# A LayerNorm one chunk later, three PSUM pairs and an earlier first weight slice in the first stage of an eight-core Trainium2 kernel

## Chip, cores and metric

The kernel runs on all eight cores of one Trainium2 chip. Each core does the same program on its own sequence. The time is device microseconds (us) of the slowest core. Most runs agree within 0.3%. Some runs fall into a slower state, in which some cores show a lower granted clock (0.811 to 0.959 where the fast runs show 0.984 to 0.997) and the time is longer (a run of before with cores 2 and 3 at 0.958 and 0.959 took 862.52 us, where the fast median was 838.60; its slowest, with cores 4 to 7 at 0.815 to 0.841, took 990.49); those runs are listed but not compared. A "fast run" below is one outside that state.

## The reference, cut to what matters

One layer of a decoder. Only its first step matters here: RMSNorm of the input, the projection `v`, Gelu, and a LayerNorm of the result, for 2,112 rows per core. The change is about the order in which that is done.

```python
h = rms_norm(x, norm_g)                       # x: 2048 + 64 rows of 1024 per core
z = jnp.einsum('bld,de->ble', h, w_in)        # split into u, v, gates, ...
v_a = layer_norm(jax.nn.gelu(v_a), ln_v_g, ln_v_b)
s = chunk_spatial_mix(v_a, w_s, b_s)          # within chunks of 128 rows
y_a = gelu(u_a) * s * silu(gate_a)
# ... branch B, the merge, the output projection and the embedding: not touched
```

## The kernel before: the parts that matter

The first stage takes the rows in 17 chunks of 128 (the last has 64). One chunk passes through every engine. The names below are used through the whole text.

```python
def A0(c):      # ScalarE: square of x with its sum ("square c"); POOL: add, pow -> RMSNorm factor ("rstd c")
def A2(c):      # VectorE: x * rstd * norm_g -> bf16                          ("scale c")
def A3(c):      # TensorE: 8 transposes into one PSUM bank
def A4(c):      # VectorE: copy of that bank into HT                          ("HT copy c")
def Bmm(c, slots):                    # TensorE: 4 matmuls for each slot (a slice of w_v): 16 in all
def Bact_g(c):  # ScalarE: Gelu of the PSUM pair, with its sum                ("Gelu c")
def Bact_s(c):  # ScalarE: square of that, with its sum
def C1(c):      # VectorE: three 1-element steps: mean, mean^2 - eps, variance ("the scalars")
def C2(c):      # POOL:    pow(variance, -1/2), one element per row           ("the pow")
def C3(c):      # VectorE: one 1-element step, then the normalise, 1024 wide
# C1, C2 and C3 are the LayerNorm of a chunk, "LN c".
```

The helper `S.op`, on which these functions rest, adds the semaphore waits that the data need. What an engine has to do is called its queue here, and the order of these calls in the program is taken as the order in each queue. PSUM is what the traces call `ps`, where every matmul of these traces puts its result (`MATMUL ps<-WR,HT`); a pair is two of its banks. `okc(c)` says that chunk c exists.

```python
        for i in range(4, NCH + 5):
            if 5 <= i - 1 < NCH:
                A2(i - 1)
            if 3 <= i - 3 < NCH:
                Bmm(i - 3, (0, 1))
            if 4 <= i - 2 < NCH:
                A3(i - 2)
                A4(i - 2)
            if 3 <= i - 3 < NCH:
                Bmm(i - 3, (2, 3))
            if okc(i - 5):
                C1(i - 5)
                C2(i - 5)
            if okc(i - 4):
                Bact_g(i - 4)
            if 5 <= i + 1 < NCH:
                A0(i + 1)
            if okc(i - 4):
                Bact_s(i - 4)
            if okc(i - 5):
                C3(i - 5)
            # ... loads cut
            if i == 13:
                S.op("dve", CP(Bd[:, :], ps[3][:, :]), reads=[B_bank[6], B_bank[7]], writes=[B_Bd])
            if i == 12:
                make_Bd()      # 16 small matmuls into ps[3], used later
                # ... loads cut
```

After this loop the second stage begins. It starts with the projection of `u` ("u-projection"), whose TensorE work needs all HT copies. Later, its products with `VA` need every LN.

Of the kernel before, what the change touches and what calls it, by code (L numbers as in the profile page):

```python
# [15 lines left out]
NCH = 17  # L16
# [145 lines left out]
def CP(out, in_):  # L162
    return lambda e: e.tensor_copy(out=out, in_=in_)  # L163
# [4 lines left out]
def DMA(out, in_):  # L168
    return lambda e: e.dma_start(out=out, in_=in_)  # L169

def build_program(stop_after=99, dbg=()):
# [31 lines left out]
    with ExitStack() as es:  # L203
# [90 lines left out]
        def warm(n):  # L294
            S.group("pe", [MM(ps[2][:, 512:1024], JUNK[:, 0:128], JUNK[:, 0:512], True, True) for _ in range(n)], reads=[B_junk])
# [58 lines left out]
        def A0(c):  # L354
            r, sl, hs = crow(c), c % NXI, c % 3
            S.op("act", ACT(HTOK[hs][0:r, :], XIN[sl][0:r, :], AF.Square, scale=1.0 / 32, accum_out=st(c, 0, r)),
                 reads=[B_xin[sl]], writes=[B_htok[hs], B_stat[c]])
            S.op("pool", TT(st(c, 1), st(c, 0), cc(C_EPS), ALU.add), reads=[B_cst], writes=[B_stat[c]])
            S.op("pool", TT(st(c, 2), st(c, 1), cc(C_NH), ALU.pow), reads=[B_cst], writes=[B_stat[c]])

        def A2(c):
            r, sl, hs = crow(c), c % NXI, c % 3
            S.op("dve", STT(HTOK[hs][0:r, :], XIN[sl][0:r, :], st(c, 2, r), BC0[0:r, :], ALU.mult, ALU.mult),
                 reads=[B_xin[sl], B_stat[c]] + B_bc0h, writes=[B_htok[hs]])

        def A3(c):
            r, sl, hs = crow(c), c % 2, c % 3
            pt = bank_bf(sl)
            S.group("pe", [TR(pt[:, k * 128:k * 128 + r], HTOK[hs][0:r, k * 128:(k + 1) * 128], ident[0:r, 0:r])
                           for k in range(8)], reads=[B_htok[hs], B_identb], writes=[B_bank[sl]])  # L370

        def A4(c):
            r, t0, sl = crow(c), c * 128, c % 2
            pt = bank_bf(sl)
            S.op("dve", CP(HT3[:, :, t0:t0 + r], pt.rearrange("p (k t) -> p k t", t=128)[:, :, 0:r]),
                 reads=[B_bank[sl]], writes=[B_hT[c]])

        def v_pair(c):
            return 1 + c if c < 3 else 1 + (c + 1) % 2

        def Bmm(c, slots=(0, 1, 2, 3)):
            r, t0, pi = crow(c), c * 128, v_pair(c)
            fns = [MM(ps[pi][0:r, q * 512:(q + 1) * 512], HT[:, k * NT + t0:k * NT + t0 + r],
                      WR[:, k * D + q * 512:k * D + (q + 1) * 512], k == 0, k == 7)
                   for s_ in slots for k in (2 * s_, 2 * s_ + 1) for q in range(2)]
            if slots[0] == 0:
                S._waits("pe", (), [B_bank[2 * pi], B_bank[2 * pi + 1]])
            S.group("pe", fns, reads=[B_hT[c]] + [B_ring[s_] for s_ in slots],
                    writes=[B_bank[2 * pi], B_bank[2 * pi + 1]] if slots[-1] == 3 else [])

        def Bact_g(c):
            r, pi, gs = crow(c), v_pair(c), c % 4
            S.op("act", ACT(GV[gs][0:r, :], ps[pi][0:r, :], AF.Gelu_apprx_tanh, accum_out=st(c, 3, r)),
                 reads=[B_bank[2 * pi], B_bank[2 * pi + 1]], writes=[B_gv[gs], B_stat[c]])

        def Bact_s(c):
            r, gs = crow(c), c % 4
            gv = GV[gs]
            S.op("act", ACT(JUNK[0:r, :], gv[0:r, :], AF.Square, accum_out=st(c, 4, r)),
                 reads=[B_gv[gs]], writes=[B_junk, B_stat[c]])  # L400

        def C1(c):
            r = crow(c)
            S.op("dve", TS(st(c, 5, r), st(c, 3, r), INVD, None, ALU.mult), writes=[B_stat[c]])
            S.op("dve", TS(st(c, 6, r), st(c, 5, r), st(c, 5, r), -LN_EPS, ALU.mult, ALU.add), writes=[B_stat[c]])
            S.op("dve", STT(st(c, 9, r), st(c, 4, r), INVD, st(c, 6, r), ALU.mult, ALU.subtract), writes=[B_stat[c]])

        def C2(c):
            S.op("pool", TT(st(c, 10), st(c, 9), cc(C_NH), ALU.pow), reads=[B_cst], writes=[B_stat[c]])
# [3 lines left out]
        def make_Bd():  # L413
            for q in range(2):
                fns = []
                for h in range(4 * q, 4 * q + 4):
                    o = ps[3][:, h * 128:(h + 1) * 128]
                    fns.append(MM(o, BC2b[:, h * 128:(h + 1) * 128], wT[:, h * 128:(h + 1) * 128], True, False))
                    fns.append(MM(o, ones[0:1, :], bsr[0:1, h * 128:(h + 1) * 128], False, True))
                S.group("pe", fns, reads=[B_bc2b, B_wT, B_ones, B_bsr], writes=[B_bank[6 + q]])  # L420

        def C3(c):
            r, gs = crow(c), c % 4
            gv = GV[gs]
            va = VA[0:r, c * D:(c + 1) * D]
            S.op("dve", STT(st(c, 12, r), st(c, 5, r), -1.0, st(c, 10, r), ALU.mult, ALU.mult), writes=[B_stat[c]])
            S.op("dve", TS(va, gv[0:r, :], st(c, 10, r), st(c, 12, r), ALU.mult, ALU.add),
                 reads=[B_stat[c], B_gv[gs]], writes=[B_va[c]])
            if c >= 15:
                S.op("dve", TS(gv[0:r, :], gv[0:r, :], st(c, 10, r), st(c, 12, r), ALU.mult, ALU.add),  # L430
                     reads=[B_stat[c]], writes=[B_gv[gs]])
                S.op("dve", TT(gv[0:r, :], gv[0:r, :], BC1[0:r, :], ALU.mult), reads=[B_bc1], writes=[B_gv[gs]])
                S.op("dve", TT(gv[0:r, :], gv[0:r, :], BC2[0:r, :], ALU.add), reads=[B_bc2], writes=[B_gv[gs]])
                dst = vp_d if c == 15 else vs_d
                ob = Buf("vout%d" % c)
                S.dma("sp", [DMA(dst[:, :], gv[0:r, :])], ob, reads=[B_gv[gs]])
                out_bufs.append(ob)

        def okc(c):
            return 0 <= c < NCH  # L440
# [13 lines left out]
                 writes=[B_bc0h[q]])  # L454
        warm(9)
        A2(0)
        A2(1)
        A3(0)
        A4(0)
        A3(1)  # L460
        A4(1)
        for s_ in range(2):
            for c in range(2):
                Bmm(c, (s_,))
        A2(2)
        A3(2)
        A4(2)
# [10 lines left out]
        A2(3)  # L478
        for c in range(3):
            Bmm(c, (2,))  # L480
        A0(4)
        Bmm(0, (3,))
        Bmm(1, (3,))
        A3(3)
        A4(3)
        Bmm(2, (3,))
        A2(4)
        for i in range(4, NCH + 5):
            if 5 <= i - 1 < NCH:
                A2(i - 1)  # L490
            if 3 <= i - 3 < NCH:
# [3 lines that stand above are left out]
                A4(i - 2)  # L495
            if 3 <= i - 3 < NCH:
                Bmm(i - 3, (2, 3))
            if okc(i - 5):
                C1(i - 5)
                C2(i - 5)  # L500
            if okc(i - 4):
                Bact_g(i - 4)
            if 5 <= i + 1 < NCH:
                A0(i + 1)
            if okc(i - 4):
                Bact_s(i - 4)
            if okc(i - 5):
                C3(i - 5)
            if NXI + 3 <= i + 5 < NCH:
                x_load(i + 5)  # L510
            if i == 9:
                S.op("pool", lambda e: e.affine_select(out=wT3, in_=WST.rearrange("s (h t) -> s h t", t=128),
                                                       pattern=[[0, 8], [1, 128]], compare_op=ALU.is_ge, fill=0.0,
                                                       base=0, channel_multiplier=-1),
                     reads=[B_ws], writes=[B_wT])
                issue_loads(6)
            if i == 11:
                issue_loads(NRING)
            if i == 10:
                S.op("dve", CP(BC2b, BC2), reads=[B_bc2], writes=[B_bc2b])  # L520
            if i == 13:
                S.op("dve", CP(Bd[:, :], ps[3][:, :]), reads=[B_bank[6], B_bank[7]], writes=[B_Bd])
            if i == 12:
                make_Bd()
                S.dma("sp", [DMA(BC1, ln_g_d.partition_broadcast(128))], B_bc1, writes=[B_bc1])
                S.dma("pool", [DMA(WPP[:, :].rearrange("p (k c) -> p k c", c=D),
                                   w_pp_d.rearrange("(k p) c -> p k c", p=128))], B_wpp, writes=[B_wpp])
            if i == 14:
                emit_blk_dmas()
                S.dma("sp", [DMA(ci_s[:, :], ci0_d[:, :])], B_cis[0], writes=B_cis)  # L530
# [495 lines left out]
```

## Time and profile before

| | before |
|---|---|
| time, median of 3 runs | 838.74 us (838.24 to 839.37) |
| spans of the eight cores in the profiled run | 832.9 to 836.9 us, mean 834.8 |
| u-projection starts, mean of the cores | 98.0 us |

How to read the lines: in a page, each engine has its busy time, the share of the span and the number of instructions. In the chain of waits (the line with shares only) each part of the span goes to the engine that the end of the program had to wait for. PE is TensorE, DVE is VectorE, ACT is ScalarE, POOL is GpSimd. The page of the kernel before, the slowest core (core 7):

```profile
span 836.9 us, 14194 instructions; the slowest of 8 cores (832.9 to 836.9 us)
...
PE 810.0 (97%) x4569; PEld 431.7 (52%) x4569; DVE 445.8 (53%) x726; ACT 301.0 (36%) x517; POOL 116.6 (14%) x257
...
PE 88%; DMA 3%; issue 3%; DVE 3%; ACT 1%; POOL 1%; DVEq 0%; POOLq 0%; SPq 0%; ACTq 0%
```

TensorE is busy 97% of the time. The rest must be sought where TensorE waits. All but 3.8 us of its waiting (on core 7) is in the first stage. In the list of waits of core 3 (columns: waited for, us in total, times, longest) its largest entry is this:

```profile
PE ps L143 <- DVE stat L159: 6.7, 10, 2.4
```

"DVE stat L159" is the VectorE instruction that began when the wait ended (at 34.88 us, for a matmul at 35.11). What TensorE needs is the end of the one before it, an HT copy (34.28 to 34.96). The timeline of core 3 shows it. Its columns are start, length, engine, line, operation, output, input, shape, count, and in brackets the idle time of the engine before it with what ended it. TensorE of before:

```profile
30.79 1.89 PE L143 MATMUL ps<-WR,HT 128*128 128x512 bf16 x8
35.11 1.89 PE L143 MATMUL ps<-WR,HT 128*128 128x512 bf16 x8 [2.43 <-DVE stat L159]
...
39.43 1.89 PE L143 MATMUL ps<-WR,HT 128*128 128x512 bf16 x8 [0.26 <-DVE stat L159]
...
43.75 1.89 PE L143 MATMUL ps<-WR,HT 128*128 128x512 bf16 x8 [0.26 <-DVE stat L159]
```

TensorE waits 2.43 us once, at chunk 4, and then 0.26 us per chunk. The first instructions of successive chunks (35.11, 39.43, 43.75) lie 4.32 us apart. VectorE of before, on the same core:

```profile
30.55 0.15 DVE L159 TENSOR_SCALAR stat<-stat 128x1 f32<-128x1 f32 x1 [0.70 <-ACT SCR L149]
30.81 0.21 DVE L160 TENSOR_SCALAR stat<-stat 128x1 f32<-128x1 f32 x1
31.13 0.16 DVE L155 SCALAR_TENSOR_TENSOR stat<-stat 128x1 f32<-128x1 f32 x1
32.09 0.16 DVE L155 SCALAR_TENSOR_TENSOR stat<-stat 128x1 f32<-128x1 f32 x1 [0.80 <-POOL stat L152]
32.35 0.81 DVE L160 TENSOR_SCALAR VA<-YA,stat 128x1024 bf16<-128x1024 f32 x1
33.08 1.28 DVE L155 SCALAR_TENSOR_TENSOR YA<-MG,stat 128x1024 bf16<-128x1024 f32 x1
34.28 0.68 DVE L163 COPY HT<-ps 128x1024 bf16<-128x1024 bf16 x1
...
38.60 0.68 DVE L163 COPY HT<-ps 128x1024 bf16<-128x1024 bf16 x1
...
72.15 0.69 DVE L163 COPY HT<-ps 128x1024 bf16<-128x1024 bf16 x1 [6.08 <-PE ps L146]
...
74.30 0.16 DVE L155 SCALAR_TENSOR_TENSOR stat<-stat 128x1 f32<-128x1 f32 x1 [0.82 <-POOL stat L152]
...
75.30 1.22 DVE L163 COPY Bd<-ps 128x1024 f32<-128x1024 f32 x1
```

The first three lines are the scalars of LN 0. They waited 0.70 us for ScalarE's square. Then VectorE stands still for 0.80 us until POOL has done the pow (32.09). Normalise (32.35), scale 5 (33.08) and HT copy 4 (34.28) come behind it. TensorE's matmul at 35.11 is released by that copy. HT copy 5 follows at 38.60. The last three lines are from the stretch in which TensorE makes `Bd`: VectorE is idle 6.08 us. Only then, in the next iteration, it waits 0.82 us for the pow of LN 8 and copies `Bd` for 1.22 us.

### The profile page before, as it was taken

To read this page: it belongs to the slowest core of one execution; us is meant where nothing else is said; L and a number is where in the kernel's file an instruction comes from. 1 tells how busy PE (TensorE), PEld (TensorE's weight loads), DVE (VectorE), ACT (ScalarE), POOL (GpSimd) and SP (SyncE) were. 2 spreads that over 40 slices of the span, in tenths; PEclk is the share of its full clock that TensorE was granted. 3 is DMA by queue.
4 is the path that set the end of the run, shared out by engine and by line. 5 is a ranking of instruction groups with operands and counts; after the bars stand their busy time and mean duration, and the time that the engine had idled before them with its cause. 6 is when DMAs were issued, how large, how long until landed. Compare 5 with 4: busy or idle time off the path is not lost.

```text
span 836.9 us, 14194 instructions; the slowest of 8 cores (832.9 to 836.9 us)
## 1 busy us (share of the span) xinstructions
PE 810.0 (97%) x4569; PEld 431.7 (52%) x4569; DVE 445.8 (53%) x726; ACT 301.0 (36%) x517; POOL 116.6 (14%) x257
## 2 busy tenths in 40 slices
PE   6899999999999999999999999999999999999994
PEld 2445455555554555455555545554555454444441
DVE  4575666546565555555555322232333246777774
ACT  2675554554432332232332111111111115555552
POOL 4342210000000100101001001000010013323331
PEclk8998999999999999999999999999999999999998
DMA  8977072311300410600602406006023563444311
GB/s 180 237 178 144 1 151 39 51 24 29 51 1 1 71 31 1 101 1 2 101 1 48 86 1 101 2 0 101 2 39 62 83 171 126 142 142 143 120 76 63
DMA packets 21338, 60.78 MB, mean 73 GB/s; under 512 B 2770, under 2 KB 7058, under 8 KB 21268
## 3 DMA queue, kind: packets, MB, share of 16 engines
q0 software_dynamic: 10352, 29.89, 21.5%
q1 hardware_dynamic: 10914, 29.99, 11.5%
q8 instruction: 40, 0.66, 0.3%
q14 instruction: 30, 0.25, 0.1%
q10 hardware_dynamic: 2, 0.00, 0.0%
HBM read 78.08 MB, written 9.58 MB: 105 GB/s over the span
## 4 chain that ended last, share of the span: by engine, by line
PE 88%; DMA 3%; issue 3%; DVE 3%; ACT 1%; POOL 1%; DVEq 0%; POOLq 0%; SPq 0%; ACTq 0%
PE ps L143 86%; DMA MG<-x 2%; PE ps L146 1%; DMA YA<-pe_g 1%; POOL stat L152 1%; DVE HT L163 1%; DVE YA L155 1%; ACT YA L149 0%; ACT SCR L149 0%; DVE stat L155 0%; DVE MG L155 0%; DVE stat L160 0%; ACT MG L149 0%; POOL WR L169 0%; DVE YA L152 0%
## 5 line engine op out<-in xcount | busy, mean ns | idle before, releaser
L143 PE MATMUL ps<-HT,WR 128*128 128x512 bf16 (+2 forms) x2560 | 469.7, 342 | 0.0
L143 PEld LDWEIGHTS ps<-HT,WR 128*128 128x128 bf16 x2560 | 248.4, 98 | 200.7 <-issue 0.4
L149 ACT ACTIVATE SCR<-ps 128x512 f32<-128x512 f32 (+2 forms) x240 | 123.7, 520 | 324.1 <-PE ps L143 274.0
L155 DVE SCALAR_TENSOR_TENSOR SCR<-SCR,ps 128x512 f32<-128x512 f32 (+2 forms) x80 | 47.6, 594 | 151.1 <-PE ps L143 151.1
L152 POOL TENSOR_TENSOR stat<-stat,cst 128x1 f32<-128x1 f32 x119 | 68.2, 576 | 175.3 <-ACT SCR L149 102.9
L143 PE MATMUL ps<-WR,HT 128*128 128x512 bf16 (+1 forms) x272 | 68.8, 404 | 6.6 <-DVE stat L159 5.5
L152 DVE TENSOR_TENSOR SCR<-SCR,ps 128x512 f32<-128x512 f32 (+2 forms) x88 | 48.2, 547 | 46.3 <-PE ps L143 38.5
L155 DVE SCALAR_TENSOR_TENSOR SCR<-SCR,cpks 128x512 f32<-128x512 f32 (+1 forms) x80 | 51.6, 645 | 37.6 <-ACT SCR L149 27.8
L143 PE MATMUL ps<-HT 128*128 128x512 bf16 (+1 forms) x272 | 61.6, 379 | 2.3 <-ACT HT L149 2.3
L143 PE MATMUL ps<-YA,WR 128*128 128x512 bf16 (+2 forms) x320 | 63.6, 342 | 0.0
L143 PE MATMUL ps<-VA,WR 128*128 128x512 bf16 (+2 forms) x320 | 63.6, 342 | 0.0
L169 POOL DMA_DIRECT2D WR<-wt x44 | 24.0, 546 | 274.2 <-PE ps L143 272.4
L143 PE MATMUL ps<-WR,MG 128*128 128x512 bf16 (+1 forms) x272 | 61.3, 379 | 0.0
L143 PEld LDWEIGHTS ps<-WR,HT 128*128 128x128 bf16 (+1 forms) x272 | 26.6, 103 | 40.9 <-issue 18.1
L149 ACT ACTIVATE SCR<-SCR,cpks 128x512 f32<-128x512 f32 (+1 forms) x40 | 25.5, 637 | 60.5 <-DVE SCR L152 60.5
L152 DVE TENSOR_TENSOR SCR<-SCR 128x512 f32<-128x512 f32 (+2 forms) x40 | 23.7, 593 | 41.3 <-ACT SCR L149 41.3
L143 PEld LDWEIGHTS ps<-YA,WR 128*128 128x128 bf16 x320 | 31.3, 98 | 25.8
L143 PEld LDWEIGHTS ps<-VA,WR 128*128 128x128 bf16 x320 | 31.3, 98 | 25.8
L143 PEld LDWEIGHTS ps<-WR,MG 128*128 128x128 bf16 (+1 forms) x272 | 26.7, 99 | 31.7 <-issue 0.4
L143 PEld LDWEIGHTS ps<-HT 128*128 128x128 bf16 (+1 forms) x272 | 26.0, 99 | 31.1 <-issue 3.3
L155 DVE SCALAR_TENSOR_TENSOR YA<-YA,ps 128x1024 f32<-128x1024 f32 (+1 forms) x17 | 20.7, 1220 | 21.7 <-ACT YA L149 21.7
L152 DVE TENSOR_TENSOR VA<-SCR 128x512 bf16<-128x512 f32 (+2 forms) x48 | 25.3, 526 | 8.1 <-DVE SCR L152 4.8
(85 smaller groups left out, 549.2 us busy)
## 6 DMA issues: line engine op xcount, KB each, us to landing
WR<-wt POOLq DMA_DIRECT2D x44, 512.0 KB, 10.2
y<-YA SPq DMA_DIRECT2D x16, 512.0 KB, 2.9
MG<-x SPq DMA_DIRECT2D x12, 512.0 KB, 7.8
WR<-x SPq DMA_DIRECT2D x8, 512.0 KB, 4.8
VA<-x SPq DMA_DIRECT2D x8, 512.0 KB, 4.4
WR<-w_v POOLq DMA_DIRECT2D x4, 512.0 KB, 11.6
MG<-x POOLq DMA_DIRECT2D x4, 512.0 KB, 13.4
SCR<-p SPq DMA_DIRECT2D x16, 128.0 KB, 4.3
```

Of the source, the lines that this page charges most:

```text
L143: return lambda e: e.matmul(out, lhsT=lhsT, rhs=rhs, start=start, stop=stop)
L146: return lambda e: e.transpose(out, in_, idn)
L149: return lambda e: e.activation(out=out, in_=in_, func=func, **kw)
L152: return lambda e: e.tensor_tensor(out=out, in0=in0, in1=in1, op=op)
L155: return lambda e: e.scalar_tensor_tensor(out=out, in0=in0, scalar=scalar, in1=in1, op0=op0, op1=op1)
L163: return lambda e: e.tensor_copy(out=out, in_=in_)
L169: return lambda e: e.dma_start(out=out, in_=in_)
```

## The change

The change has four intents.

1. LayerNorm one chunk later in VectorE's queue, so that no scale or HT copy stands behind a LayerNorm that waits for ScalarE.
2. Three PSUM pairs in turn, and Gelu 0 ahead of square 4.
3. The copy of `Bd` while TensorE still makes it.
4. The first slice of weights used for chunk 0 before chunk 1 is ready.
5. The consequence: C2 now comes behind A0 of chunk i+1 in the program, and so in POOL's queue.

```diff
@@ -378,3 +378,3 @@
         def v_pair(c):
-            return 1 + c if c < 3 else 1 + (c + 1) % 2
+            return 1 + c % 3
 
@@ -456,10 +456,13 @@
         A2(0)
-        A2(1)
         A3(0)
         A4(0)
+        warm(2)
+        Bmm(0, (0,))
+        A2(1)
         A3(1)
         A4(1)
-        for s_ in range(2):
-            for c in range(2):
-                Bmm(c, (s_,))
+        warm(2)
+        Bmm(1, (0,))
+        for c in range(2):
+            Bmm(c, (1,))
         A2(2)
@@ -480,4 +483,5 @@
             Bmm(c, (2,))
-        A0(4)
         Bmm(0, (3,))
+        Bact_g(0)
+        A0(4)
         Bmm(1, (3,))
@@ -487,3 +491,3 @@
         A2(4)
-        for i in range(4, NCH + 5):
+        for i in range(4, NCH + 7):
             if 5 <= i - 1 < NCH:
@@ -497,6 +501,3 @@
                 Bmm(i - 3, (2, 3))
-            if okc(i - 5):
-                C1(i - 5)
-                C2(i - 5)
-            if okc(i - 4):
+            if 1 <= i - 4 < NCH:
                 Bact_g(i - 4)
@@ -504,6 +505,8 @@
                 A0(i + 1)
-            if okc(i - 4):
-                Bact_s(i - 4)
             if okc(i - 5):
-                C3(i - 5)
+                Bact_s(i - 5)
+            if okc(i - 6):
+                C1(i - 6)
+                C2(i - 6)
+                C3(i - 6)
             if NXI + 3 <= i + 5 < NCH:
@@ -520,6 +523,5 @@
                 S.op("dve", CP(BC2b, BC2), reads=[B_bc2], writes=[B_bc2b])
-            if i == 13:
-                S.op("dve", CP(Bd[:, :], ps[3][:, :]), reads=[B_bank[6], B_bank[7]], writes=[B_Bd])
             if i == 12:
                 make_Bd()
+                S.op("dve", CP(Bd[:, :], ps[3][:, :]), reads=[B_bank[6], B_bank[7]], writes=[B_Bd])
                 S.dma("sp", [DMA(BC1, ln_g_d.partition_broadcast(128))], B_bc1, writes=[B_bc1])
```

More of the change, by code (lines that the diff above doesn't have):

```diff
@@ L480, in build_program @@
             Bmm(c, (2,))
+        Bmm(0, (3,))
+        Bact_g(0)
         A0(4)
-        Bmm(0, (3,))
         Bmm(1, (3,))
```

## The prediction

> **What bounds the kernel now.** The page has TensorE busy 97% of the span; the chain that ended last is 86% matmuls. From 97-99 us on TensorE waits for others only 3.8 us in all (list of waits). So only the first stage (to 96.7-99.3 us by core) has slack. There, one chunk costs TensorE 3.89 us (16 matmuls at 216 ns, 8 transposes 0.44 us), but the timeline repeats every 4.32 us, set by VectorE's queue: scale 1.20, HT copy 0.60, three LayerNorm scalars 0.9, a wait of 0.80 for POOL's pow, one scalar 0.27, the 1024-wide normalise 0.73. TensorE's waits in this stage are for the HT copy (shown as "DVE stat L159"): 0.26 us per chunk, and 2.44 us once, at 32.7 us (seven of eight cores within 0.1): scale 5 stands in VectorE's queue behind LayerNorm 0, which waited for ScalarE's square.
>
> **What the change does.**
> 1. *LayerNorm a chunk later.* VectorE's order and work per chunk stay, so the 4.32 us period stays. The 2.44 us wait goes: scale 5 and the HT copy of chunk 4 no longer wait for ScalarE. Core 7 should also lose the half-rate stretch behind it (35-38.8 us, about 1.7 us lost). [...] the trace shows such half-rate stretches (matmul spacing 427 ns for 216), but after 2.4 us of idling cores 1 to 5 show none.
> 2. *Three pairs.* No wait for a PSUM pair shows in the steady chunks, so nothing. Gelu of chunk 0 ahead of the square of chunk 4 removes a 0.5-1.0 us wait for ACT at 28 us, but the next transpose needs x of chunk 4 (lands 26.1) and waits instead: nothing.
> 3. *Bd copy in iteration 12* runs while TensorE makes Bd (5.3 us, VectorE idle 5.8): 1.13 us off VectorE's limiting queue.
> 4. *Early slice.* The fourth weight slice lands near 24.4 us anyway (waits on w_v of 0.3-0.8 us): about 0.
> 5. *Cost:* POOL now takes the rstd of chunk i+1 before LayerNorm's pow. Where TensorE sets the pace (after Bd) that delays VectorE about 0.7 us once.
> 6. *Cost:* one more LayerNorm (2.5 us) remains after the last HT copy. VectorE then reaches the second stage about 14.9 us after TensorE starts it (12.3 now; 111.58 against 99.27), and the fifth spatial product needs the bank that the first eviction frees; I estimate a new TensorE wait of about 1.3 us near 110 us.
>
> **Sum** (cores 1-3): 2.4 + 1.1 - 0.6 = about 3 us off the first stage, 1.3 given back; core 7 perhaps 2 more. Slowest cores are now 836.1-836.9.
>
> **Prediction: 836.2 us, range 833.0 to 838.8. Faster by over 2%: 0.01; within 2%: 0.98; slower by over 2%: 0.01.**
>
> **What would show it.** Right: the wait of 2.44 us gone; period of the HT copies still 4.3 us; u-projection starts 3-5 us earlier (95-96 on core 3); the Bd copy inside the Bd matmuls; a new TensorE wait for VectorE near 110 us, about 1 us. Wrong: period near 3.9 us (VectorE did not bound); no wait at 110; half-rate stretches elsewhere.
>
> **What would make it wrong.** Half-rate clock windows falling differently (each costs up to 1.7 us); POOL's order delaying every chunk instead of one (0.7 us each, ten chunks: slower by several us); later landing of slices or x.

The sum: 2.4 + 1.1 - 0.6, about 3 us off the first stage, 1.3 given back, and perhaps 2 more on core 7. The 2 us of core 7 were the author's estimate, from the 1.7 us that this core lost at half rate behind its wait (granted clock 0.50 from 35.5 to 38.7 us); that the stretch would go with the wait was not shown.

## Result, and the profile after

| | before | after |
|---|---|---|
| median of fast runs (4 each; before's three and a fourth) | 839.06 us | 841.36 us |
| their range | 838.24 to 840.68 | 840.78 to 841.80 |
| spans in the profiled run | 832.9 to 836.9 | 836.9 to 839.2 |

The ratio after over before is 1.0025, with a 95% interval of 1.0007 to 1.0042. (A ratio here is the mean time of one kernel's fast runs over that of the other's fast runs of the same rounds. So it is not quite the ratio of the medians.) The change is a loss of a quarter of a per cent, where a gain of 0.3% was predicted.

The page of the kernel after, the slowest core (core 3):

```profile
span 839.2 us, 14221 instructions; the slowest of 8 cores (836.9 to 839.2 us)
...
PE 809.2 (96%) x4573; PEld 430.6 (51%) x4573; DVE 446.0 (53%) x726; ACT 300.6 (36%) x517; POOL 116.2 (14%) x257
...
PE 85%; DVE 5%; issue 3%; DMA 3%; POOL 2%; ACT 1%; DVEq 0%; POOLq 0%; SPq 0%; ACTq 0%
```

The busy time of TensorE is as before, and the chain has lost matmul share to DVE and POOL. Where the time went is seen by milestones. The table has means over the eight cores of each profiled run, in us from the span's start.

| | before | after | difference |
|---|---|---|---|
| HT copy 4 starts | 33.98 | 32.83 | -1.15 |
| HT copy 5 starts | 38.40 | 39.41 | +1.01 |
| TensorE begins to make `Bd` | 61.89 | 63.80 | +1.91 |
| u-projection starts | 98.01 | 99.80 | +1.79 |
| new TensorE wait early in the second stage | 0 | 1.29 | +1.29 |
| span | 834.84 | 837.90 | +3.06 |

The gain at chunk 4 came. It was lost, and more, within the next chunk: a swing of 2.16 us between two HT copies. The last rows add up: 1.79 + 1.29 = 3.08, and the span grew by 3.06. So the whole difference arises before about 117 us.

VectorE after, core 3 (to be held against the same lines of before):

```profile
31.40 1.28 DVE L155 SCALAR_TENSOR_TENSOR YA<-MG,stat 128x1024 bf16<-128x1024 f32 x1 [0.58 <-POOL stat L152]
32.60 0.68 DVE L163 COPY HT<-ps 128x1024 bf16<-128x1024 bf16 x1
34.03 0.15 DVE L159 TENSOR_SCALAR stat<-stat 128x1 f32<-128x1 f32 x1 [0.75 <-ACT SCR L149]
34.29 0.21 DVE L160 TENSOR_SCALAR stat<-stat 128x1 f32<-128x1 f32 x1
34.61 0.16 DVE L155 SCALAR_TENSOR_TENSOR stat<-stat 128x1 f32<-128x1 f32 x1
38.02 0.16 DVE L155 SCALAR_TENSOR_TENSOR stat<-stat 128x1 f32<-128x1 f32 x1 [3.25 <-POOL stat L152]
38.29 0.81 DVE L160 TENSOR_SCALAR VA<-YA,stat 128x1024 bf16<-128x1024 f32 x1
39.02 1.27 DVE L155 SCALAR_TENSOR_TENSOR MG<-MG,stat 128x1024 bf16<-128x1024 f32 x1
40.22 0.68 DVE L163 COPY HT<-ps 128x1024 bf16<-128x1024 bf16 x1
...
69.61 1.22 DVE L163 COPY Bd<-ps 128x1024 f32<-128x1024 f32 x1 [3.04 <-PE ps L143]
...
76.63 0.16 DVE L155 SCALAR_TENSOR_TENSOR stat<-stat 128x1 f32<-128x1 f32 x1 [1.47 <-POOL stat L152]
```

HT copy 4 is at 32.60, 1.7 us earlier than before: the wait at chunk 4 is gone. LN 0 comes next. Its scalars are done at 34.77 (34.61 + 0.16). Then VectorE waits 3.25 us for POOL, where it was 0.80 us before. HT copy 5 stands behind this and comes at 40.22 instead of 38.60. On cores 1, 2, 5 and 7 the wait is 2.6 us, on cores 0, 3, 4 and 6 it is 3.0 to 3.25. On these last four, square 6 had itself begun 0.3 to 1.35 us late (on three of them it waited for the DMA of x), and square 7 comes behind it; on the others it had not. The Bd copy now runs at 69.61, in what was idle time, as intended. The last line shows that LN 7 waits 1.47 us for POOL, against 0.82 us at the like place before: this is the extra 0.7 us that the prediction did expect.

What POOL does in those 3.25 us stands in its own timeline, after, core 3:

```profile
33.02 0.88 POOL L152 TENSOR_TENSOR stat<-stat,cst 128x1 f32<-128x1 f32 x2 [1.80 <-ACT MG L149]
36.11 1.40 POOL L152 TENSOR_TENSOR stat<-stat,cst 128x1 f32<-128x1 f32 x3 [2.21 <-ACT MG L149]
```

Nothing, until 36.11. Then it does three instructions in a row: add and pow for rstd 7, and only then the pow of LN 0. The input of that pow had been ready since 34.77. Rstd 7 waits for ScalarE (the releaser in the bracket is "ACT MG L149", a square of x). ScalarE after, core 3:

```profile
33.83 1.00 ACT L149 ACTIVATE YA<-ps 128x1024 f32<-128x1024 f32 x1
...
34.83 1.05 ACT L149 ACTIVATE MG<-MG 128x1024 bf16<-128x1024 f32 x1
35.78 0.19 ACT L149 ACTIVATION_READ_ACCUMULATOR MG<-MG 128x1 f32 x1
```

The first line is Gelu 2, the second square 7, the third the reading of its sum, which ends at 35.97. So the pow of LN 0, half a microsecond of work, stood behind a square that ScalarE had not begun when LN 0 asked for its pow. A ready instruction was not taken for 1.3 us (34.77 to 36.11), in which POOL stood idle, because one ahead of it in the queue was not ready.

TensorE after, core 3:

```profile
35.60 1.89 PE L143 MATMUL ps<-WR,HT 128*128 128x512 bf16 x8
41.04 1.89 PE L143 MATMUL ps<-WR,HT 128*128 128x512 bf16 x8 [3.56 <-DVE stat L159]
...
117.04 0.27 PE L143 MATMUL ps<-wT,VA 128*128 128x128 bf16 x2 [1.29 <-DVE SCR L155]
```

The 2.43 us wait at 35.11 is now a 3.56 us wait at 41.04. On cores 1, 2, 5 and 7 it is 2.1 us and on 0, 4 and 6 2.5 to 3.2. The last line is the new wait of the second stage, where it needs what VectorE has not yet evicted. The list of waits of core 3 after has both:

```profile
PE ps L143 <- DVE stat L159: 7.5, 9, 3.6
...
PE ps L143 <- DVE SCR L155: 1.3, 1, 1.3
```

The wait for "DVE SCR L155" of 1.3 us is new, and it is on every core (1.28 to 1.30).

Where does the rest of the loss between HT copy 5 and `Bd` (+0.90) come from? From the clock. Between 30 and 80 us the clock is at 1.00 or at 0.50 in the traces of before and after (before, core 7: 0.50 from 35.5 to 38.7 us, 1.00 from 39 to 60), so the granted clock of a window gives the time at half rate ((1 - clock) x 2 x length). Between 30 and 60 us, cores 0, 6 and 7 have one such stretch of about 3.4 us before (clock 0.66 from 34 to 39 us). After, it is cores 0, 2, 4, 6 and 7 (clock 0.76 from 39 to 46 us). The three of before lie mostly ahead of HT copy 5, the five of after all lie behind it. From HT copy 5 to `Bd` the three cores without one in after (1, 3 and 5) take only 0.1 us longer than before, and the five with one 0.9 to 2.4 us longer. The 2.4 us are core 6. There the queue fault came twice: VectorE waited 3.34 us for the pow of LN 1 as well, where it was 0.80 us before. Which core gets a stretch can't be told from its wait: core 3 with 3.56 us of waiting had none in that window, and core 7 with 2.08 us did.

### The profile page after: what moved, and what is told of

The parts are those of the page before. It is cut to its first block, busy times and chain, and to the rows that moved or that the text cites. A ratio compares the mean times of both kernels' runs of the same rounds, so it can differ in the third digit from the quotient of the medians.

```text
span 839.2 us, 14221 instructions; the slowest of 8 cores (836.9 to 839.2 us)
## 1 busy us (share of the span) xinstructions
PE 809.2 (96%) x4573; PEld 430.6 (51%) x4573; DVE 446.0 (53%) x726; ACT 300.6 (36%) x517; POOL 116.2 (14%) x257
## 4 chain that ended last, share of the span: by engine, by line
PE 85%; DVE 5%; issue 3%; DMA 3%; POOL 2%; ACT 1%; DVEq 0%; POOLq 0%; SPq 0%; ACTq 0%
PE ps L143 84%; DMA WR<-w_v 2%; POOL stat L152 1%; PE ps L146 1%; DMA YA<-pe_g 1%; DVE MG L155 1%; DVE HT L163 1%; DMA MG<-x 1%; DVE stat L155 1%; DVE YA L155 0%; DVE YA L152 0%; ACT YA L149 0%; DVE VA L160 0%; DVE stat L160 0%; ACT SCR L149 0%
## 5 line engine op out<-in xcount | busy, mean ns | idle before, releaser
L149 ACT ACTIVATE SCR<-ps 128x512 f32<-128x512 f32 (+2 forms) x240 | 123.7, 521 | 324.4 <-PE ps L143 269.3
L155 DVE SCALAR_TENSOR_TENSOR SCR<-SCR,ps 128x512 f32<-128x512 f32 (+2 forms) x80 | 47.6, 595 | 151.1 <-PE ps L143 151.1
L143 PE MATMUL ps<-WR,HT 128*128 128x512 bf16 (+1 forms) x272 | 66.4, 390 | 10.0 <-DVE stat L159 7.5
L155 DVE SCALAR_TENSOR_TENSOR SCR<-SCR,cpks 128x512 f32<-128x512 f32 (+1 forms) x80 | 51.6, 645 | 38.0 <-ACT SCR L149 28.2
L149 ACT ACTIVATE SCR<-SCR,cpks 128x512 f32<-128x512 f32 (+1 forms) x40 | 25.5, 638 | 60.9 <-DVE SCR L152 60.9
L155 DVE SCALAR_TENSOR_TENSOR YA<-YA,ps 128x1024 f32<-128x1024 f32 (+1 forms) x17 | 20.7, 1220 | 20.5 <-ACT YA L149 20.5
```

The lines of the kernel that those rows point to most:

```text
L143: return lambda e: e.matmul(out, lhsT=lhsT, rhs=rhs, start=start, stop=stop)
L149: return lambda e: e.activation(out=out, in_=in_, func=func, **kw)
L155: return lambda e: e.scalar_tensor_tensor(out=out, in0=in0, scalar=scalar, in1=in1, op0=op0, op1=op1)
```

## The experiments

The first call had four kernels that take the change apart. The second had the reverse of the suspected cause, a test of the tail, and two more (f3 and g1). The third had four that settle leftovers. Each call shared one chip and the runs of the kernel before: 11 runs each, of which 11, 8 and 9 were fast, with fast medians of 839.21, 839.24 and 838.60 us. Every kernel gave a correct result. Where an expectation names a theory by a letter, P is the place of the pow in POOL's queue, L the LayerNorm part of the change as a whole, and T the LayerNorm that is left over at the end of the stage. The rivals were that the early slice of weights or the third pair cost the time, or that the half-rate stretches alone did.

All numbers, ratios against before of the same rounds with 95% intervals. The start of the u-projection is the mean of the eight cores in the one profiled run. "New wait" is TensorE's in the second stage.

| kernel | fast runs: median | ratio | u-projection starts | new wait |
|---|---|---|---|---|
| before (prediction's rounds) | 839.06 | 1 | 98.0 | 0 |
| after | 841.36 | 1.0025 [1.0007, 1.0042] | 99.8 | 1.29 |
| e1_pow_first | 838.16 | 0.9992 [0.9972, 1.0011] | 96.1 | 1.29 |
| e2_ln_as_before | 837.34 | 0.9975 [0.9959, 0.9991] | 97.1 | 0 |
| e3_slice_alone | 839.00 | 0.9995 [0.9979, 1.0012] | 98.7 | 0 |
| e4_bd_alone | 838.07 | 0.9983 [0.9966, 0.9999] | 97.0 | 0 |
| f1_pow_last | 842.93 | 1.0045 [1.0023, 1.0067] | 102.8 | 0 |
| f2_catch_up | 836.28 | 0.9964 [0.9943, 0.9986] | 96.5 | 0 |
| f3_square4_first | 839.08 | 0.9996 [0.9979, 1.0013] | 96.4 | 1.30 |
| f4_two_pairs | 838.25 | 0.9992 [0.9979, 1.0004] | 96.5 | 1.29 |
| g1_split | 832.82 (2 runs) | 0.9920 [0.9886, 0.9954] | 91.3 | 0.45 |
| g3_split_catch_up | 831.46 | 0.9920 [0.9902, 0.9938] | 90.9 | 0 |
| g4_old_start | 830.88 | 0.9906 [0.9892, 0.9919] | 90.1 | 0 |
| h1_normalise_later | 831.83 | 0.9926 [0.9908, 0.9943] | 91.7 | 0 |

### e1_pow_first: after, with the pow ahead of rstd again

```diff
@@ -501,2 +501,5 @@
                 Bmm(i - 3, (2, 3))
+            if okc(i - 6):
+                C1(i - 6)
+                C2(i - 6)
             if 1 <= i - 4 < NCH:
@@ -508,4 +511,2 @@
             if okc(i - 6):
-                C1(i - 6)
-                C2(i - 6)
                 C3(i - 6)
```

> The changed kernel, with the three LayerNorm scalars and POOL's pow of chunk i-6 queued ahead of the Gelu and the square of chunk i+1 (as the kernel before orders them), normalise where it was. Theory P (POOL order): in the changed kernel LayerNorm 0's pow stood in POOL's queue behind the rstd of chunk 7, which waits for ScalarE's square of chunk 7, so VectorE waited 2.6 to 3.3 us for POOL near 36 us and TensorE then 2.1 to 3.6 us for the HT copy of chunk 5. Then here VectorE's wait for POOL falls to 0.8 us, TensorE's wait there to about 0.3 us (1.7 at most), the u projection starts on the mean of 8 cores at about 97.5 us (changed kernel 99.8, before 98.0), the wait of 1.29 us near 116 us stays, and the time is about 839.3. Rival S (ScalarE is late with the squares of LayerNorm itself): the wait only moves to the first LayerNorm scalar, TensorE's wait stays above 1.8 us on all cores, start at 99.5 or later, time 841.

The median of five fast runs is 838.16 us (a sixth was slow, 945.37). That is 3 us less than after (2.8 us by the two ratios, which compare each with before in its own call). VectorE of core 3:

```profile
33.64 0.16 DVE L155 SCALAR_TENSOR_TENSOR stat<-stat 128x1 f32<-128x1 f32 x1
35.01 0.16 DVE L155 SCALAR_TENSOR_TENSOR stat<-stat 128x1 f32<-128x1 f32 x1 [1.20 <-POOL stat L152]
...
37.20 0.69 DVE L163 COPY HT<-ps 128x1024 bf16<-128x1024 bf16 x1
```

The wait for POOL is 1.20 us instead of 3.25, and HT copy 5 comes at 37.20 instead of 40.22. (About 1 us of that is not the order: in this run square 6 of core 3 was not late, and the scalars of LN 0 are done 1 us earlier. The means are below.) TensorE of core 3:

```profile
38.03 1.89 PE L143 MATMUL ps<-WR,HT 128*128 128x512 bf16 x8 [0.68 <-DVE stat L159]
...
42.72 1.89 PE L143 MATMUL ps<-WR,HT 128*128 128x512 bf16 x8 [0.62 <-DVE stat L159]
```

What was one wait of 3.56 us is two of 0.68 and 0.62. The longest single wait between 28 and 48 us is 0.8 to 1.6 us, by core, and no core has a half-rate stretch between 30 and 60 us. The new wait of the second stage stays, 1.29 us on every core. So moving two calls up by some lines takes back the loss and nothing else: theory P holds. Rival S, that ScalarE is late with LayerNorm's own squares, expected TensorE's wait to stay above 1.8 us and fails. The sizes were not all as expected: VectorE still waits 1.20 us for the pow where 0.8 was expected, and the u-projection starts at 96.1 us on the mean where 97.5 was. The gain has two parts. On the mean HT copy 5 comes 1.75 us earlier than in after (37.66 for 39.41). And there is less time at half rate (none for 2.1 us between 30 and 60 us, 3.4 for 5.1 us between 60 and 80 us), which is worth half of the difference, 1.9 us. Together that is the 3.7 us by which the u-projection starts earlier. Core 3 begins the u-projection at 95.74, which is inside what had been predicted for the whole change (95 to 96).

### e2_ln_as_before: after, with the LayerNorm as before

```diff
@@ -491,3 +491,3 @@
         A2(4)
-        for i in range(4, NCH + 7):
+        for i in range(4, NCH + 5):
             if 5 <= i - 1 < NCH:
@@ -501,2 +501,5 @@
                 Bmm(i - 3, (2, 3))
+            if okc(i - 5):
+                C1(i - 5)
+                C2(i - 5)
             if 1 <= i - 4 < NCH:
@@ -505,8 +508,6 @@
                 A0(i + 1)
+            if okc(i - 4):
+                Bact_s(i - 4)
             if okc(i - 5):
-                Bact_s(i - 5)
-            if okc(i - 6):
-                C1(i - 6)
-                C2(i - 6)
-                C3(i - 6)
+                C3(i - 5)
             if NXI + 3 <= i + 5 < NCH:
```

> The changed kernel with the LayerNorm steps (squares, scalars, pow, normalise) at the lag and in the order of the kernel before; three pairs, early slice, early Gelu 0 and early Bd copy stay. Theory L (the later LayerNorm is what costs): the wait for the HT copy of chunk 4 near 33 us returns with 2.0 to 2.5 us, the ones of 2.1 to 3.6 us near 40 us and of 1.29 us near 116 us go, VectorE waits 0.8 us for each pow, u projection starts at about 97.8 us (mean of cores; 98.0 before, less 1.1 for the Bd copy, plus 0.9 for the start), time about 839, 2 us under the changed kernel. Rival (the early slice and Gelu at the start cost the time): start stays at 99.3 or later and the time within 0.7 us of the changed kernel.

837.34 us (about 839 was expected). The wait at chunk 4 is back (2.0 us on every core), and the new wait of the second stage is gone. So the other parts of the change together are worth a gain of about 2 us, and the LayerNorm part loses about 4 against that (841.36 less 837.34, medians of different calls). This is theory L. It says where the loss is, and e1 says why.

### e3_slice_alone and e4_bd_alone: two of the other parts by themselves

```diff
@@ -456,10 +456,13 @@
         A2(0)
-        A2(1)
         A3(0)
         A4(0)
+        warm(2)
+        Bmm(0, (0,))
+        A2(1)
         A3(1)
         A4(1)
-        for s_ in range(2):
-            for c in range(2):
-                Bmm(c, (s_,))
+        warm(2)
+        Bmm(1, (0,))
+        for c in range(2):
+            Bmm(c, (1,))
         A2(2)
```

> The kernel before with the early slice alone (chunk 0 through transpose, HT copy and four matmuls before chunk 1's scale, two times two warm matmuls). My prediction had about 0 for it. Reading now: in the changed kernel the scale of chunk 4 starts at 29.8 us for 28.6, part of it from this. Expected if it costs: start of the 28 matmuls after chunk 2 at 20.2 to 20.9 us on all cores, u projection 0.4 to 0.9 us later than before in the mean (98.4 to 98.9), time plus 0.5. If it is neutral: within 0.3 us of 98.0 after allowing for half-rate stretches of the clock (each 3.4 us long, worth up to 1.7 us on one core).

```diff
@@ -520,6 +520,5 @@
                 S.op("dve", CP(BC2b, BC2), reads=[B_bc2], writes=[B_bc2b])
-            if i == 13:
-                S.op("dve", CP(Bd[:, :], ps[3][:, :]), reads=[B_bank[6], B_bank[7]], writes=[B_Bd])
             if i == 12:
                 make_Bd()
+                S.op("dve", CP(Bd[:, :], ps[3][:, :]), reads=[B_bank[6], B_bank[7]], writes=[B_Bd])
                 S.dma("sp", [DMA(BC1, ln_g_d.partition_broadcast(128))], B_bc1, writes=[B_bc1])
```

> The kernel before with the Bd copy alone moved to iteration 12. Expected as predicted: the copy of 1.22 us runs right behind the Bd matmuls while VectorE idles, HT copies 12 and later are 1.1 us earlier against the end of the Bd matmuls, u projection starts at about 96.9 us (mean of cores), no wait near 116 us, time about 837.9 (ratio 0.9987). Rival: scale 12 now queues behind the copy and the HT copy of chunk 11 is late by as much, so no change (98.0, ratio 1.000).

The early slice alone is neutral: 839.00 us against 839.21. Its u-projection starts 0.66 us later in the profiled run. The cores there had 6.0 us at half rate between 60 and 80 us where before has 5.1, so most of that may be chance. Below about 0.7 us this part stays unresolved. The Bd copy alone starts the u-projection 1.0 us earlier and takes 1.1 us off the median, as its 1.22 us in VectorE's queue had promised.

### f1_pow_last: before, with the pow behind rstd (the reverse of e1)

```diff
@@ -499,3 +499,2 @@
                 C1(i - 5)
-                C2(i - 5)
             if okc(i - 4):
@@ -504,2 +503,4 @@
                 A0(i + 1)
+            if okc(i - 5):
+                C2(i - 5)
             if okc(i - 4):
```

> The reverse of e1: the kernel before with one edit, POOL's pow of LayerNorm i-5 queued behind the rstd of chunk i+1. Theory P: at the start LayerNorm 0's pow waits for the rstd of chunk 6 (in the kernel before that rstd ends at about 33.5 us), so VectorE's wait for POOL near 32 us grows from 0.8 to about 3.4 us, TensorE's wait near 35 us from 2.44 to about 5 us [...], the u projection starts 2.5 to 4 us later than before (mean 100.5 to 102) and the time is 841.7 to 843. If POOL's order is harmless without the later LayerNorm: 98.0 and 839.

This is the suspected cause alone, put into the kernel before. Nothing else is changed, the lag of LayerNorm least of all. VectorE of core 3, to be held against 31.13, 32.09 and 34.28 of before:

```profile
31.30 0.16 DVE L155 SCALAR_TENSOR_TENSOR stat<-stat 128x1 f32<-128x1 f32 x1
34.35 0.16 DVE L155 SCALAR_TENSOR_TENSOR stat<-stat 128x1 f32<-128x1 f32 x1 [2.90 <-POOL stat L152]
...
36.55 0.68 DVE L163 COPY HT<-ps 128x1024 bf16<-128x1024 bf16 x1
```

The wait for POOL grows from 0.80 to 2.90 us and HT copy 4 comes 2.3 us later. POOL again stands idle until square 6 is done (32.85), with the scalars of LN 0 done at 31.46. TensorE of core 3:

```profile
37.38 3.57 PE L143 MATMUL ps<-WR,HT 128*128 128x512 bf16 x8 [4.55 <-DVE stat L159]
40.74 1.06 PE L146 MATMUL ps<-ident,YA 128*128 128x128 bf16 x8
```

It waits 4.55 us where before waits 2.43 (4.47 to 4.71 on all cores). The eight matmuls behind that wait take 3.57 us where the same eight take 1.89 us in before: TensorE runs at half rate (the granted clock of this core is 0.89 on the mean of 30 to 60 us, which makes 6.6 us at half rate). All eight cores have one or two such stretches between 30 and 60 us (3.4 or 6.8 us; mean 4.7 us, where before has 1.3). The time is 842.93 us, the ratio 1.0045. The u-projection starts 4.8 us later than before, more than expected: 2.4 us are there at HT copy 4 (means), and the additional time at half rate up to 80 us is worth 2.3 us. So the order in POOL's queue makes a loss in either kernel, and theory P holds from both sides. The half-rate stretches come with the wait here: all eight cores have one after 4.47 to 4.71 us of waiting, three have one in before after 2.36 to 2.44 us, and none has one in e1, whose longest wait between 28 and 48 us is 1.6 us. So they are taken as an addition to the wait and not as a rival to it. That is the author's reading; no run varies the clock alone.

### f2_catch_up: e1, with the lag taken back while TensorE makes Bd

```diff
@@ -491,3 +491,3 @@
         A2(4)
-        for i in range(4, NCH + 7):
+        for i in range(4, NCH + 5):
             if 5 <= i - 1 < NCH:
@@ -501,5 +501,6 @@
                 Bmm(i - 3, (2, 3))
-            if okc(i - 6):
-                C1(i - 6)
-                C2(i - 6)
+            lag = 6 if i <= 12 else 5
+            if okc(i - lag):
+                C1(i - lag)
+                C2(i - lag)
             if 1 <= i - 4 < NCH:
@@ -508,6 +509,11 @@
                 A0(i + 1)
-            if okc(i - 5):
-                Bact_s(i - 5)
-            if okc(i - 6):
-                C3(i - 6)
+            for c in ((i - 5,) if i < 12 else (7, 8) if i == 12 else (i - 4,)):
+                if okc(c):
+                    Bact_s(c)
+            if okc(i - lag):
+                C3(i - lag)
+            if i == 12:
+                C1(7)
+                C2(7)
+                C3(7)
             if NXI + 3 <= i + 5 < NCH:
```

> e1 with the lag taken back while VectorE idles during the Bd matmuls: LayerNorm 6 and 7 both in iteration 12, lag of before from there on. Theory T (the 1.29 us wait near 112-117 us comes from the one LayerNorm more after the last HT copy): wait gone, u projection starts as in e1 (96.1 mean), time 837.1, 1.2 under e1. If the wait comes from the three pairs or from TensorE arriving earlier: it stays at 1 us or more.

Two LayerNorms are done in iteration 12, where VectorE is idle, and the lag is that of before afterwards. TensorE of core 3 at the place of the new wait:

```profile
112.02 9.04 PE L143 MATMUL ps<-HT,WR 128*128 128x512 bf16 x48
```

48 matmuls without a gap. The new wait is gone on all cores, so it is the left-over LayerNorm that causes it: theory T holds. The median is 836.28 us, 1.9 us less than e1 but in another call. In the profiled runs the u-projection starts 0.4 us later than in e1 and the mean span is 0.5 us shorter, so the gain in time is not well measured.

### f3_square4_first and f4_two_pairs: two details of e1 undone

```diff
@@ -484,4 +484,4 @@
         Bmm(0, (3,))
-        Bact_g(0)
         A0(4)
+        Bact_g(0)
         Bmm(1, (3,))
```

> e1 with ScalarE's square of chunk 4 ahead of Gelu 0, as in the kernel before. The changed kernel's scale of chunk 4 started at 29.8 us for 28.6 before, and TensorE waited 0.8 us for it (transposes of chunk 4 at 31.2 for 30.3). If the Gelu ahead of the square costs: scale 4 starts 0.9 to 1.2 us earlier, that wait of 0.8 us goes or turns into the wait for ACT of 0.5 to 1.0 us that the kernel before has at 28 us, and the HT copy of chunk 4 is at 31.9 instead of 32.8 us; the u projection starts 0.5 us earlier than in e1 at most (HT copy of chunk 5 then waits for LayerNorm 0), time 838 plus or minus 0.5. If neutral: as e1.

```diff
@@ -378,3 +378,3 @@
         def v_pair(c):
-            return 1 + c % 3
+            return 1 + c if c < 3 else 1 + (c + 1) % 2
 
```

> e1 with the PSUM pairs of the kernel before (two alternate from chunk 3 on). My prediction had nothing for the third pair. Then all is as in e1: u projection starts at 96.1 us in the mean (half-rate stretches may move it by 1), TensorE shows no wait for ScalarE (for a pair's release) above 0.3 us between 30 and 95 us, time 838.4 plus or minus 0.6. If the third pair gives something: waits for ACT appear, start 97 or later, time 839.5 or more.

With square 4 first, HT copy 4 is 0.6 us earlier (mean 32.06 against 32.64), but the waits at the next chunk grow from 1.6 to 1.9 us in sum and only 0.25 us is left when TensorE begins to make `Bd` (61.23 against 61.48) and nothing at the u-projection (96.4 against 96.1), where f3 had more time at half rate (4.7 against 3.4 us between 60 and 80 us). Undoing the third pair changes nothing: 838.25 against 838.16 us. So the third pair gives nothing in this form, as had been predicted.

### g1_split: e1, with the normalise behind the next chunk's scalars

```diff
@@ -491,3 +491,3 @@
         A2(4)
-        for i in range(4, NCH + 7):
+        for i in range(4, NCH + 8):
             if 5 <= i - 1 < NCH:
@@ -504,2 +504,4 @@
                 C2(i - 6)
+            if okc(i - 7):
+                C3(i - 7)
             if 1 <= i - 4 < NCH:
@@ -510,4 +512,2 @@
                 Bact_s(i - 5)
-            if okc(i - 6):
-                C3(i - 6)
             if NXI + 3 <= i + 5 < NCH:
```

> A version to beat both: e1 with the normalise of chunk i-7 behind the LayerNorm scalars of chunk i-6, so that VectorE no longer waits for POOL's pow (0.8 us a chunk). If VectorE's 4.32 us period bounds the stage, as I predicted: period of the HT copies falls to TensorE's 3.9 us, waits of 0.26 us a chunk go, the u projection starts at 92.5 to 94.5 us (e1: 96.1), and since the LayerNorms after the last HT copy lose their pow waits as well, no wait or under 1 us near 110 us; time 835 to 836. If the period was set by something else: HT copies stay 4.3 us apart, start 96, and the wait near 112 us grows to 3 us for another LayerNorm left over: 840.

In this kernel VectorE need not stand still for the pow. It sends the variance, and does that normalise one chunk later. Only two of its seven runs were fast (831.47 and 834.16 us; slow ones from 857.31 to 993.88), so its size rests on little; the start at 91.3 us is earlier than the 92.5 to 94.5 expected. The transposes of core 3 come 3.9 us apart in the middle of the stage (43.03, 46.93, 50.88), which is TensorE's own pace, instead of 4.32, and the u-projection starts at 91.3. With h1 below, this settles that the wait for the pow, 0.80 us per chunk, was what made VectorE the slower engine.

### h1_normalise_later: before, with that one edit alone

```diff
@@ -487,3 +487,3 @@
         A2(4)
-        for i in range(4, NCH + 5):
+        for i in range(4, NCH + 6):
             if 5 <= i - 1 < NCH:
@@ -500,2 +500,4 @@
                 C2(i - 5)
+            if okc(i - 6):
+                C3(i - 6)
             if okc(i - 4):
@@ -506,4 +508,2 @@
                 Bact_s(i - 4)
-            if okc(i - 5):
-                C3(i - 5)
             if NXI + 3 <= i + 5 < NCH:
```

> The kernel before with one edit: only the normalise goes a chunk later in VectorE's queue, the scalars and the pow stay. If it is VectorE's wait for the pow in its own queue (0.8 us a chunk) and the normalise ahead of scale 5 that cost, this small edit does most of g1: wait of 2.44 us near 35 us falls to 0.5 to 1 us, HT copies come 3.9 us apart, u projection starts at 92.5 to 94 us (no early Bd copy), no wait near 107 us, time 833 to 835. If the Bd copy or the new start are needed for g1's gain: 836 to 838.

831.83 us (three fast runs of six), ratio 0.9926, where 833 to 835 us was expected. Only the normalise is a chunk later; the scalars, the pow and everything else stay. VectorE of core 3 in a steady chunk:

```profile
37.69 0.14 DVE L159 TENSOR_SCALAR stat<-stat 128x1 f32<-128x1 f32 x1
37.94 0.21 DVE L160 TENSOR_SCALAR stat<-stat 128x1 f32<-128x1 f32 x1
38.26 0.26 DVE L155 SCALAR_TENSOR_TENSOR stat<-stat 128x1 f32<-128x1 f32 x2
38.63 0.81 DVE L160 TENSOR_SCALAR VA<-YA,stat 128x1024 bf16<-128x1024 f32 x1
39.36 1.28 DVE L155 SCALAR_TENSOR_TENSOR MG<-MG,stat 128x1024 bf16<-128x1024 f32 x1
40.62 0.69 DVE L163 COPY HT<-ps 128x1024 bf16<-128x1024 bf16 x1
```

Two 1-element steps run in a row at 38.26 (x2: the last of the three scalars, and the first step of the normalise of the chunk before), with no wait for POOL in between. One chunk of this queue, 37.69 to 41.23 (the next scalars), is 3.5 us long, less than TensorE's 3.89 us per chunk. At the old place TensorE waits 0.7 us for HT copy 4 on every core, and then 0.43 us for HT copy 5 (0.62 on core 3).

### g3_split_catch_up and g4_old_start: the best versions

The first edit is against g1, the second against g3.

```diff
@@ -492 +492 @@
-        for i in range(4, NCH + 8):
+        for i in range(4, NCH + 6):
@@ -502,5 +502,6 @@
-            if okc(i - 6):
-                C1(i - 6)
-                C2(i - 6)
-            if okc(i - 7):
-                C3(i - 7)
+            lag = 6 if i <= 12 else 5
+            if okc(i - lag):
+                C1(i - lag)
+                C2(i - lag)
+            if okc(i - lag - 1):
+                C3(i - lag - 1)
@@ -511,2 +512,7 @@
-            if okc(i - 5):
-                Bact_s(i - 5)
+            for c in ((i - 5,) if i < 12 else (7, 8) if i == 12 else (i - 4,)):
+                if okc(c):
+                    Bact_s(c)
+            if i == 12:
+                C1(7)
+                C2(7)
+                C3(6)
```

> g1 (normalise one chunk behind the scalars) with the lag taken back by one chunk in iteration 12, while the Bd matmuls run. Expected: HT copies 3.9 us apart as in g1, u projection starts at 91 us (mean), the last wait of 0.45 us near 107 us gone, fast runs at 831 to 833 us (g1: 831.5 and 834.2), ratio to before 0.990 to 0.992. If the extra LayerNorm does not fit into the Bd matmuls, the HT copy of chunk 11 or 12 is late and the start is 0.5 to 1 us later.

```diff
@@ -456,0 +457 @@
+        A2(1)
@@ -459,3 +459,0 @@
-        warm(2)
-        Bmm(0, (0,))
-        A2(1)
@@ -464,4 +462,3 @@
-        warm(2)
-        Bmm(1, (0,))
-        for c in range(2):
-            Bmm(c, (1,))
+        for s_ in range(2):
+            for c in range(2):
+                Bmm(c, (s_,))
@@ -483,0 +481 @@
+        A0(4)
@@ -486 +483,0 @@
-        A0(4)
```

> g3 with the start of the kernel before (no early slice, no warm matmuls there, square of chunk 4 before Gelu 0). If the new start costs as its late scale 4 suggests (29.8 us for 28.6), the HT copy of chunk 4 is 0.5 to 1 us earlier than in g3 and the u projection starts up to 0.8 us earlier; time 831 to 832. If the fourth weight slice (about 24.5 us) and x of chunk 4 (about 26 us) pace the start in both, as predicted: within 0.4 us of g3 where no half-rate stretch differs.

g3 removes the 0.45 us wait that g1 still had: 831.46 us. g4 puts back the start of before, that is without the early slice and with square 4 ahead of Gelu 0: 830.88 us, ratio 0.9906, the fastest of all. It beats before by 0.9% and after by 10 us (medians of different calls). Its u-projection starts 0.8 us earlier than g3's, so the new start did not help here. But the fast runs of both (829.99 to 832.97 and 830.41 to 832.01) overlap, and the two edits were not taken apart.

One reservation: the four fast kernels g1, g3, g4 and h1 fell into the slow state in 12 of 24 runs, while before did in 5 of the 22 runs of the same calls. In that state they take 857 to 860 us mostly, against 862 to 866 for before, with a few far worse in either. No run here tells whether that is chance.

## Why the prediction was wrong

- **Wait at chunk 4 gone (item 1).** The 2.4 us at that place did go: HT copy 4 starts at 32.60 on core 3. But the step "the 2.44 us wait goes" was read as a gain of 2.4 us, and a wait of 2.1 to 3.6 us came at chunk 5 instead. The step that failed is item 5; item 1 is over-sized besides (see "The sum").
- **POOL's order, "about 0.7 us once", after Bd (item 5).** The place was found, but only half of what it does. The 0.7 us after `Bd` came (1.47 against 0.82). The cost at LN 0 was missed: 1.8 to 2.4 us of extra VectorE waiting (2.61 to 3.25 us for 0.80). The queue had been looked at in the steady chunks, in which rstd is done long before LayerNorm asks. At the start ScalarE has a backlog (on core 3 it goes without a gap from square 6 at 31.73 to 41.1), and there the square of chunk 7 is late. e1 took 3 us off the kernel after by this order alone. f1 put 3.7 us onto before (842.93 against 839.24) by this order alone. In both, about half of the change in the start of the u-projection is the wait itself and about half is time at half rate, of which the part after 60 us may be chance.
- **One LayerNorm more after the last HT copy (item 6).** Right in mechanism and size: 1.28 to 1.30 us on every core, at 115 to 117 us (predicted 1.3, near 110). f2 shows its cause.
- **Bd copy (item 3).** Right: 1.13 us predicted, 1.0 us earlier in e4.
- **Three pairs, Gelu first, early slice (items 2 and 4).** "Nothing" was right for the pairs (f4), and for the slice within the noise (e3). "Waits instead: nothing" for Gelu first was half right: scale 4 is 1.0 us later (29.53 against 28.56 on core 3) and TensorE waits 0.79 us at its transposes. Hardly any of that is left later in the stage (f3).
- **Period of 4.32 us.** Right: it stays in after, and g1 and h1 show that it falls to about 3.9 when the wait for the pow is taken out, so VectorE did set it. A 128x1 pow took 0.55 us on POOL (31.44 us on core 3 of before), and VectorE stood still 0.80 us for it, from its last scalar to the next.
- **The sum.** Without the queue fault, the u-projection of e1 starts 1.9 us earlier on average (3.2 on core 3), where about 3 were expected, and its time is 0.1% below before, within noise. So even then the forecast gain was too large, and the part that was too large is item 1's 2.4 us. In e1 TensorE begins to make `Bd` at 61.48 us on the mean, only 0.4 us before the 61.89 of before, and e4, whose program is that of before up to there, had 62.24, so even 0.4 is hardly clear of chance. What the wait gave was taken elsewhere: HT copy 4 is 1.3 us earlier and not 2.4 (32.64 against 33.98), as scale 4 comes later (item 2), and VectorE's waits for the pows of LN 0 and LN 1 (1.20 and 1.16 us for 0.80) take another 0.8. The rest of the 1.9 us is the `Bd` copy (1.0 in e4) and the clock: 3.4 us at half rate between 60 and 80 us where before has 5.1.
- **Half-rate stretches.** They were named as what could make it wrong, and five cores had one instead of three. e1, with the short waits, had none there. They account for nearly all of the 0.9 us between HT copy 5 and `Bd`: the three cores without one lost 0.1 us there. What the traces of before and after show of them between 30 and 80 us: a stretch is 3.4 or 6.8 us long at a granted clock of 0.50 (core 7 of before from 35.5 to 38.7 us, core 3 from 65.4 to 71.9), and 128x512 matmuls are 427 ns apart in it, for 216. The wait ahead of one does not tell whether it comes. After 2.1 us of waiting cores 2 and 7 of after had one and cores 1 and 5 had none, and core 3 had none after 3.56 us. Between 60 and 80 us, around and after the 16 matmuls for `Bd` (4.7 to 6.1 us without a gap, half of them with a single row and in fp32), seven cores or more of before, after and f1 had 3.4 or 6.8 us at half rate. That these matmuls are the reason is the author's estimate, from the place alone; no run leaves them out.

## What to carry to other kernels

When steps are moved, list for every in-order queue what now stands ahead of each of them, the engine with the smallest work included, and check it at the start of a stage, where other engines may have a backlog (here ScalarE, without a gap from 31.73 to 41.1 us), as well as in the steady part. To hide a latency between engines, move only the step that consumes the answer (here the normalise: one edit, 0.7%) and leave the step that asks for it early. Work that is put off may have to be paid at the stage's end (here 1.29 us of TensorE's time, in after and e1) unless it is taken back in a stretch where its engine is idle (f2: no such wait).
